# Moving the key transposes of an RWKV recurrence back in TensorE's order, in a hybrid attention, RWKV and mixture-of-experts layer

## Chip, cores and metric

The kernel runs on 1 core of one Trainium2 chip, as one launch. The metric is device time in microseconds; a run's number is the time of that core from the start to the end of the execution. The program is written against a tile framework that orders each engine's instructions when the program is built; on the chip that order is fixed, and semaphores alone hold an instruction back.

## The reference, cut to what matters

One layer on 1024 tokens of width 1024, all in float32:

```python
h = rms_norm(x, norm1_gain)
p = h @ w_in                      # q, k, v of 12 heads; RWKV's r, k, v and LoRAs; two gates
y_att  = dilated_window_attention(q, k, v) @ w_att_out
y_rwkv = rwkv7_time_mix(p_rwkv, ...)          # 8 heads of 64, a scan over the tokens
x = x + (gates[:D] * y_att + gates[D:] * y_rwkv) @ w_out
x = x + hierarchical_moe(rms_norm(x, norm2_gain), ...)   # 32 experts, top 2 in one group

def step(state, inp):             # the scan of rwkv7_time_mix
    r_t, w_t, k_t, v_t, kk_t, b_t = inp
    sa = einsum('bhvk,bhk->bhv', state, -kk_t)
    state = state * w_t + sa[..., None] * b_t + v_t[..., None] * k_t
    return state, einsum('bhvk,bhk->bhv', state, r_t)
```

The scan is computed in chunks of 64 tokens: within a chunk everything is a matrix product, and only the state Z is carried from chunk to chunk.

## The kernel before

**Stages.** The input projection is made tile by tile: a tile is 128 columns of `w_in`, and each takes 48 matmuls of 128 x 128 by 128 x 512 (8 slices of the contraction, two halves of the tokens, and three products of a high and a low part, since the operands are split into two). These are the *dense matmuls* of this text, all issued in `inproj_steps` (L309). Tiles 3 to 14 are RWKV's r, k and v of four head pairs p (three tiles, 144 matmuls, a pair), then come 10 tiles of gates, then the attention's q, k, v.

**The preparation.** `prep(p)` builds, for a head pair p and for each half h of the tokens (so eight *halves* in all), what the recurrence needs, and stores it in DRAM. Its TensorE steps, in source order: projections of decay and rate (L577, L578); key norms (L583) and their spread over rows by transposes (L593); transposes of v (L597); transposes of the keys BK (L647), eight a half; the bonus product (L657, L658); the products BK x AR of each chunk (L672, 32 on the chip a half); and products of the masked result with v (L691). VectorE forms BK in four writes, L631 twice and L634 last in the trace shown; BK has one buffer, so the next half's BK can be written only when this half's transposes and products have read it. The key transposes go through PSUM tiles `pt` to the tile BT (ScalarE copies, L648) and to DRAM as dBT (SyncE's queue, L650). No other step of the preparation reads BT. VectorE cuts the products into cT, Bm and MC with masks (L681, L685, L686).

**The solve and the recurrence.** `solve(q)` inverts the chunks' triangular blocks, 31 steps on VectorE and then small matmuls (L737, L746), of which L737 stands in `tc.high_priority(offset=-400)`. After the preparation the kernel runs the second solve, and then 8 blocks of the recurrence, which load dAR, dMC, dBT and the rest (issued on POOL's queue) and run L851, L859, L867, L874 and L878, with a group norm behind each block (`gnorm`, its transposes are L810). Then come the attention, the merge, and the experts.

**Fillers.** The dense matmuls are generators in a list `fillers`. `fill(n)` issues the next n of them at that place of the source. In a half of `prep` there are 16 in front of L593, 2 + 2 + 14 between L597 and L647, and 28 behind that, 62 in all; at the start of each `prep` the rest of the pair's 144 is issued. So the source mixes 62 dense matmuls into every half.

**Order.** The source order is only a preference. Every instruction gets a number by its place in the source; when the program is built the framework steps through an estimate of the execution, and whenever an engine is free it takes, of the instructions of that engine that are ready, the one with the lowest number. `tc.high_priority(offset=-400)` adds 400 to the numbers inside it. A dense matmul far later in the source is therefore taken as soon as nothing earlier is ready.

The lines that the change touches, L643 to L650; LP is 0:

```python
            for jj in range(2):
                pt = pb([2, 2, 128])
                for j in range(2):
                    for c in range(2):
                        with tc.high_priority(offset=-LP):
                            nc.tensor.transpose(pt[:, j, c], BK[:, 2 * jj + j, 128 * c:128 * c + 128], ident)
                nc.scalar.activation(BT[:, 2 * jj:2 * jj + 2], pt, AF.Copy)
                fill(FQ)
            stq.dma_start(dBT[j0:j0 + 4, :, p].rearrange("j q m -> q j m"), BT.rearrange("q j c k -> q j (c k)"))
```

Of the kernel before, what the change touches and what calls it, by code (L numbers as in the profile page):

```python
# [26 lines left out]
FT, FS, FP, FA, GL = 20, 6, 2, 18, 10  # L27
FI, FQ, TP, FR, SQ, SG, SB, UJ, QW, QL, QT, QJ = 14, 2, 1, 16, 1, 0, 1, 1, 1, 0, 0, 1
FB = 14
LP, LB, LR, PF, MP, QB, GB, NY = 0, 0, 0, 1, 0, 1, 2, 2  # L30
DILS = (1, 4, 16)
NEG = -1e30
N_EXP = 32
# [1755 lines left out]
```

## Time and profile before

| | |
|---|---|
| median of 3 runs | 1712.75 us (1712.74 to 1716.41) |
| the profiled execution | 1709.74 us |
| its span, first to last instruction | 1708.0 us |
| TensorE busy | 1643.0 us, 96% of the span |
| VectorE busy | 1201.2 us, 70% |
| ScalarE busy | 873.0 us, 51% |
| mean granted clock of TensorE | 0.986 of full speed |

PE is TensorE, PEld its weight loads, DVE VectorE, ACT ScalarE, POOL GpSimd, SP SyncE. A row of a timeline has the start, the duration (both us), the engine and line, the operation, the tile written and the tiles read, the shape and, behind x, how many like instructions it merges; in brackets stands the idle time of the engine ahead of it and what ended it. Matmuls overlap, so the pace of a run of them is the distance of their starts, not the duration. A row of a table by stage has the stretch, its length, busy time and number of instructions of each engine, the granted clock of TensorE and the share and rate of the DMA engines. A row of waits has the waiting engine and line, what it waited for, the sum in us, how many times, and the longest.

### The profile page before, as it was taken

The page shows a single profiled execution, that of the slowest core. Times are in us where ns is not written, and L with a number is a line of the kernel's source. Part 1 is how long each engine was busy: PE and PEld are TensorE (multiplying, and loading weights), DVE is VectorE, ACT ScalarE, POOL GpSimd, SP SyncE. Part 2 cuts the span into 40 slices and gives each one's busy share as a digit, 9 for nine tenths or more (in the row PEclk, how much of TensorE's full clock was granted, in tenths as well). Part 3 has the DMA queues.
Part 4 walks back from the last instruction along what each step waited for, and adds up shares of the span by engine and source line. Part 5 has one row for each costly group of instructions (what it writes and reads, how often), then busy time and mean ns, then how long its engine had stood idle before and what let it go on. Part 6 is the DMA issues. An engine that isn't in the chain of part 4 may idle for free. (4 is left out here: it accounts for less than half of the span.)

```text
span 1708.0 us, 25910 instructions
## 1 busy us (share of the span) xinstructions
PE 1643.0 (96%) x9419; PEld 1307.3 (77%) x9420; DVE 1201.2 (70%) x2191; ACT 873.0 (51%) x1317; POOL 304.1 (18%) x338
## 2 busy tenths in 40 slices
PE   8999999999998999999999999799999999999996
PEld 6677777787776777777777777578888888888884
DVE  5648798793663445434326856699999999998985
ACT  4524443423221334343433122388888888887774
POOL 0100102223431011000112211212222212221211
PEclk9999999999998999999999999899999999999998
DMA  8334324474752121111128573689999999999993
GB/s 298 120 91 133 121 87 142 136 258 146 231 176 68 38 69 56 50 41 53 69 74 301 210 266 136 234 274 373 379 374 370 376 366 377 372 361 366 366 376 102
DMA packets 138411, 360.34 MB, mean 211 GB/s; under 512 B 15792, under 2 KB 57344, under 8 KB 138276
## 3 DMA queue, kind: packets, MB, share of 16 engines
q1 hardware_dynamic: 116140, 297.89, 47.9%
q0 software_dynamic: 17936, 56.33, 11.6%
q10 hardware_dynamic: 4200, 4.40, 0.8%
q8 instruction: 76, 1.25, 0.3%
q14 instruction: 59, 0.48, 0.1%
HBM read 304.39 MB, written 62.29 MB: 215 GB/s over the span
## 5 line engine op out<-in xcount | busy, mean ns | idle before, releaser
L1605 PE MATMUL pb<-u,xTh 128*128 128x512 f32 x1040 | 343.2, 405 | 0.5 <-ACT xTh L1600 0.5
L309 PE MATMUL pa<-xlo,wh 128*128 128x512 f32 x736 | 302.3, 411 | 0.0
L309 PE MATMUL pa<-xhi,wh 128*128 128x512 f32 x736 | 299.3, 407 | 2.9 <-DVE qT L937 1.4
L309 PE MATMUL pa<-xhi,wl 128*128 128x512 f32 x736 | 297.0, 404 | 2.3 <-DVE wl L280 2.3
L1605 PEld LDWEIGHTS pb<-u,xTh 128*128 128x128 f32 x1040 | 193.7, 189 | 41.8 <-ACT xTh L1600 1.3
L1605 PE MATMUL pb<-u,xTl 128*128 128x512 f32 x520 | 210.5, 405 | 0.0
L309 PEld LDWEIGHTS pa<-xhi,wh 128*128 128x128 f32 x736 | 140.1, 190 | 36.0 <-DVE qT L937 1.8
L309 PEld LDWEIGHTS pa<-xlo,wh 128*128 128x128 f32 x736 | 139.9, 190 | 34.9 <-issue 4.0
L309 PEld LDWEIGHTS pa<-xhi,wl 128*128 128x128 f32 x736 | 140.0, 190 | 34.1 <-DVE wl L280 3.2
L1491 DVE TENSOR_TENSOR u<-fs,u 128x1024 fp32r<-128x1024 f32 x133 | 157.3, 1219 | 8.9 <-ACT u L1490 5.9
L1491 DVE TENSOR_TENSOR u<-mix,u 128x1024 fp32r<-128x1024 f32 x128 | 151.5, 1218 | 11.3 <-ACT u L1490 9.1
L1490 ACT ACTIVATE u<-fs 128x1024 fp32r<-128x1024 f32 x133 | 137.6, 1057 | 18.0 <-PE pb L1605 11.6
L1490 ACT ACTIVATE u<-mix 128x1024 fp32r<-128x1024 f32 x128 | 133.3, 1056 | 16.6 <-PE pb L1605 8.6
L1605 PE MATMUL pa<-u,hTh 128*128 128x512 f32 x496 | 138.9, 401 | 0.1
L1012 DVE SCALAR_TENSOR_TENSOR Sb<-pb,rqk,bias 128x128 f32<-128x128 f32 (+1 forms) x96 | 35.5, 407 | 120.8 <-PE pb L1011 101.3
L1584 POOL DMA_INDIRECT out<-row,tba x30 | 82.4, 2747 | 198.0 <-ACT u L1490 174.6
L1605 PEld LDWEIGHTS pb<-u,xTl 128*128 128x128 f32 x520 | 98.0, 188 | 18.1 <-DVE xTl L1601 0.6
L1605 PEld LDWEIGHTS pa<-u,hTh 128*128 128x128 f32 x496 | 90.5, 188 | 20.7 <-DVE u L1491 1.0
L1491 DVE TENSOR_TENSOR u<-raw,u 128x1024 fp32r<-128x1024 f32 x83 | 98.3, 1219 | 7.8 <-ACT u L1490 6.8
L278 ACT ACTIVATE wh<-wr 128x1024 fp32r<-128x1024 f32 x49 | 51.8, 1056 | 96.3 <-PE pa L309 76.1
L1490 ACT ACTIVATE u<-raw 128x1024 fp32r<-128x1024 f32 x83 | 86.2, 1056 | 11.8 <-PE pb L1605 6.9
L1578 POOL DMA_INDIRECT xin<-dH,tbl x32 | 37.9, 1185 | 251.1 <-PE pb L1599 231.8
(428 smaller groups left out, 2972.5 us busy)
## 6 DMA issues: line engine op xcount, KB each, us to landing
wr<-in_w_in SPq DMA_DIRECT2D x49, 512.0 KB, 3.4
fs<-in_w_expert_up SPq DMA_DIRECT2D x46, 512.0 KB
mix<-in_w_expert_gate SPq DMA_DIRECT2D x44, 512.0 KB, 12.0
fs<-in_w_expert_gate SPq DMA_DIRECT2D x44, 512.0 KB, 11.7
fs<-in_w_expert_down SPq DMA_DIRECT2D x43, 512.0 KB, 3.8
mix<-in_w_expert_down SPq DMA_DIRECT2D x42, 512.0 KB, 11.7
mix<-in_w_expert_up SPq DMA_DIRECT2D x42, 512.0 KB
raw<-in_w_expert_down SPq DMA_DIRECT2D x32, 512.0 KB, 12.8
```

The source lines that it names most:

```text
L278: nc.scalar.activation(wh, wr, AF.Copy)
L309: nc.tensor.matmul(ps, a[:, k, :], b[:, k, hs], start=(n == 0), stop=(n == 23))
L1012: nc.vector.scalar_tensor_tensor(Sb[:, hh, 0:nk], pS[:, 0:nk], u.rn[:, 0, i, hh:hh + 1], u.bias[:, hh, 256 - nk:], op0=ALU.mult, op1=ALU.add)
L1490: nc.scalar.activation(hi, raw, AF.Copy)
L1491: nc.vector.tensor_tensor(lo, raw, hi.bitcast(F32), op=ALU.subtract)
L1578: nc.gpsimd.indirect_dma_start(out=dst, out_offset=None, in_=src, in_offset=bass.IndirectOffsetOnAxis(ap=idx, axis=0), bounds_check=S - 1, ...
L1584: nc.gpsimd.indirect_dma_start(out=out, out_offset=bass.IndirectOffsetOnAxis(ap=idx, axis=0), in_=src, in_offset=None, compute_op=ALU.add)
L1605: nc.tensor.matmul(ps, x, w, start=first, stop=last)
```

## The change

The constant LP goes from 0 to 400. The 64 key transposes get numbers that are 400 higher: among the instructions that are ready, TensorE takes them after everything up to 400 places later in the source, the dense matmuls of later tiles included. Their ScalarE copies and stores keep their own numbers, but depend on the transposes.

```diff
-LP, LB, LR, PF, MP, QB, GB, NY = 0, 0, 0, 1, 0, 1, 2, 2
+LP, LB, LR, PF, MP, QB, GB, NY = 400, 0, 0, 1, 0, 1, 2, 2
```

## Rows read from the trace of the kernel before

**Rows 1.** Page, busy time of each engine over the span.

```profile
PE 1643.0 (96%) x9419; PEld 1307.3 (77%) x9420; DVE 1201.2 (70%) x2191; ACT 873.0 (51%) x1317; POOL 304.1 (18%) x338
```

**Rows 2.** Table by stage: preparation, recurrence, and the stretch behind it.

```profile
117.00:351.00 234.00, 223.27 (x1432) 180.38 (x1433) 192.03 (x468) 101.88 (x181) 31.57 (x51) 0.99 0.38 123
...
395.00:513.00 118.00, 116.67 (x1642) 92.73 (x1641) 68.37 (x195) 35.48 (x69) 45.32 (x66) 1.00 0.61 192
513.00:530.00 17.00, 10.06 (x36) 7.62 (x35) 8.48 (x23) 1.69 (x2) 5.61 (x6) 0.70 0.38 108
```

**Rows 3.** Waits of TensorE, 117 to 351 us, the longest.

```profile
PE pb L647 <- DVE BK L634: 7.5, 6, 1.6
```

**Rows 4.** Timeline around the transposes of the second half.

```profile
159.10 0.68 DVE L634 SCALAR_TENSOR_TENSOR BK<-kk,iP 128x512 f32<-128x512 f32 x1
...
159.93 1.06 PE L647 MATMUL pb<-ident,BK 128*128 128x128 f32 x8 [1.38 <-DVE BK L634]
...
160.75 0.48 PE L657 MATMUL pb<-sg,onr 128*128 128x512 f32 x1
...
161.05 1.06 ACT L648 ACTIVATE BT<-pb 128x512 f32<-128x512 f32 x2
...
161.47 3.50 PE L672 MATMUL pb<-AR,BK 64*128 64x128 f32 x32
...
162.84 1.22 DVE L280 TENSOR_TENSOR wl<-wr,wh 128x1024 fp32r<-128x1024 f32 x1
...
164.09 0.93 DVE L681 TENSOR_TENSOR cT<-pb,cv 32x128 f32<-32x128 f32 x3
...
165.23 0.40 PE L309 MATMUL pa<-xhi,wh 128*128 128x512 f32 x1
...
166.40 0.40 PE L309 MATMUL pa<-xhi,wl 128*128 128x512 f32 x1
```

**Rows 5.** L309 alone, from the start to L647 of five halves.

```profile
0.00:133.60 133.60, 70.93 (x289) 0.99 0.50 167
0.00:186.80 186.80, 103.17 (x415) 0.99 0.47 158
0.00:212.00 212.00, 117.91 (x473) 0.99 0.46 154
0.00:238.60 238.60, 135.44 (x543) 0.99 0.45 149
0.00:340.90 340.90, 198.36 (x781) 0.99 0.42 141
```

**Rows 6.** Timeline, the second solve: YT and the first product that reads it.

```profile
383.35 2.13 DVE L724 STREAM_TRANSPOSE YT<-M 128x1024 f32<-128x1024 f32 x1
...
391.43 0.24 PE L737 MATMUL pb<-YT,LW 32*32 32x32 f32 x2
```

**Rows 7.** Timeline: transposes of the third half, first BK write of the fourth.

```profile
186.84 1.06 PE L647 MATMUL pb<-ident,BK 128*128 128x128 f32 x8 [1.58 <-DVE BK L634]
...
209.27 0.75 DVE L631 TENSOR_TENSOR BK<-tc,iP 128x256 f32<-128x256 f32 x2
```

**Rows 8.** Timeline: the first product of the recurrence.

```profile
395.45 0.96 PE L851 MATMUL pb<-Z,ARs 64*64 64x64 f32 x16
```

**Rows 9.** Waits of VectorE for TensorE, 117 to 351 us.

```profile
DVE cT L681 <- PE pb L672: 2.9, 5, 0.7
...
DVE tb L660 <- PE pb L658: 1.2, 2, 0.6
```

**Rows 10.** Timeline behind the recurrence, TensorE.

```profile
521.78 1.12 PE L810 MATMUL pb<-ident,gyc 128*128 128x128 f32 x4 [5.50 <-POOL gyc L805]
524.34 0.79 PE L309 MATMUL pa<-xhi,wh 128*128 128x512 f32 x1 [1.44 <-DVE qT L937]
524.93 0.63 PE L309 MATMUL pa<-xlo,wh 128*128 128x512 f32 x1
...
528.34 0.63 PE L309 MATMUL pa<-xhi,wh 128*128 128x512 f32 x1
```

## Prediction

> **What bounds the kernel now.** I read the page first, then a table by stage, then who waited for whom in the stage that holds the change, then the timeline of one half. In [rows 1] TensorE is busy for 1643.0 of 1708.0 us, so a change of order that removes no TensorE work can only win back its idle time, 65 us in all. [rows 2] cut the early part into stages. The stage of the change (117 to 351 us, eight "halves": four head pairs p, two halves of the sequence each) leaves TensorE idle for 234.00 - 223.27 = 10.7 us; the recurrence stage (395 to 513) for 1.3 us; the short stretch behind it (513 to 530) for 6.9 us, at a mean granted clock of 0.70.
>
> Who is waited for in the first of these: [rows 3] put 7.5 us of the 10.7, in six waits, on the first key transpose of a half (L647), which waits for the last write of BK on VectorE (L634). [rows 4] show one of these: VectorE ends BK at 159.10 + 0.68, the transposes start at 159.93 after 1.38 us of idle TensorE, then come the two bonus matmuls (L657, L658), then the BK x AR products (L672), then dense matmuls again. The reader is to see two things there. The dense matmuls stand behind the whole block, although they need none of it. And the instruction next in line that matters, L672, reads BK as well.
>
> So a half is a loop through two resources: TensorE work, and a chain BK, L672, masks on VectorE, L691, the next half's projections, the next BK. Dense matmuls fill what the chain leaves free.
>
> **The change, part by part.** It alters no instruction, only the place of 64 transposes (8 a half) in TensorE's order, and with them the 16 ScalarE copies (L648) and 8 SyncE stores of dBT, which follow their transposes. Nothing is added or removed.
>
> *What leaves the front of the block.* Eight transposes take from 159.93 to the next instruction at 160.75: 0.82 us a half, 8 x 0.82 = 6.6 us in all. They must still run, so TensorE's total stays; only the chain can get shorter.
>
> *What happens to the 7.5 us of waiting.* Products L672 keep their priority and need the same write of BK, and the dense matmuls that TensorE runs at that moment are far later in the source than L672 (next paragraph), so L672 is the next to be chosen when BK is ready. I expect the same wait with L672's name on it: 0 us won. The bounds are 0 and 7.5 us (if something else took its place); I take 0, since [rows 4] show L672 right behind. The rows show TensorE idle ahead of L647 with dense work queued behind it. The Trainium skill, "TensorE: Matmul & The Clock Gate", section "Part 2: What happens when you issue a matmul", says that matmuls stay in program order and that only weight loads are pulled ahead; by that rule, which speaks against reading the 7.5 us as a gain, a wait changes its owner and the sum for it is 0, without it 7.5 us.
>
> *Where the transposes go.* The offset puts each one 400 instructions later in preference. A half issues by the source 118 instructions of its own, 62 dense matmuls and some 14 for their evacuation and weights, 194 together; two halves with the 20 dense matmuls between two preps are slightly over 400. So a transpose yields to dense matmuls up to some 138 later in the source. How far the dense stream is already ahead is a count: by the source 144 + 34 = 178 dense matmuls stand before the first half's transposes, 432 + 34 = 466 before those of the fifth, 576 + 96 = 672 before the last; [rows 5] have 289, 543 and 781, so it is ahead by 111, 77 and 109 (93 in the third half: 415 against 322). The transposes then fall back by about 138 less this, 27 to 61 dense matmuls. One takes (166.40 - 165.23) / 5 = 0.234 us [rows 4], so 6 to 14 us. An existing instruction with the same offset agrees: YT is finished at 383.35 + 2.13 = 385.48, and its first user L737 runs at 391.43, 6 us later [rows 6].
>
> *What waits for them there.* BK has one buffer, so the next half's first write (L631) waits for them: from 186.84 to 209.27 there are 22.4 us [rows 7], and 473 - 415 = 58 dense matmuls [rows 5]. Mostly covered; the fifth half, at 61 before the extra instructions of the solve (which shorten its reach), is near the edge. The stores of dBT are read back for the recurrence, whose first product stands at 395.45 [rows 8]; the last half's transposes, put back by 138 - 109 = 29 to at worst 138 dense matmuls (7 to 32 us after 341), end 20 us before that, so the store and the load behind them have time. On ScalarE the two copies cost 1.06 us [rows 4] and may stand before the next half's key norm (L588): between 0 and 1.06 us a half. I take 0, since ScalarE is busy in 101.88 of 234 us [rows 2]; in all 8 halves it would be 8.5 us.
>
> *What the shorter block gives the chain.* The products start up to 0.82 us earlier. That helps only where VectorE stood waiting for them. [rows 9]: it waited for L672 2.9 us in five waits (0.7 at most, so each is below 0.82), and 1.2 us for L658. In the other three halves it did not wait; in [rows 4] it is at a weight split (L280) when the products arrive and turns to them at 164.09 only. Below: 0 us. Above: 6.6 us. I take 2.9 us, the waits on L672; those on L658 stay, because the bonus matmuls may now fall behind the products.
>
> *Where it comes out.* TensorE loses no work, so 2.9 us must be taken from idle time. The dense matmuls left over, 2.9 / 0.234 = 12, are used up later, and the only idle time of size is behind the recurrence: 5.50 us before L810 and 1.44 before the next dense matmul [rows 10]. There is room for them.
>
> The sum on the profiled execution, span 1708.0 and 1709.74 with what lies around it: 1709.74 - 2.9 = 1706.8. The median of the runs shown, 1712.75, is 3.0 above that execution; on it, 1709.9.
>
> **The rivals.**
> *A, the forecast:* a small gain, 1709.9; its own range is 1707.6 to 1713.
>
> *B, the whole block comes off the chain.* For it: three of the six waits are in halves where VectorE is full only because of how its queue happened to be ordered; with products 0.82 us earlier the order may change too. Then 6.6 us, and the idle time behind the recurrence nearly closes. Behind that idle time the rows show the lower of the two clock levels: from 524.93 to 528.34 eight dense matmuls take 0.426 us each instead of 0.234 [rows 10]; ten at that pace cost 1.9 us, which would be saved. 1712.75 - 8.5 = 1704.3. The Trainium skill, same page, section "Part 1: The HAM clock gate (the "warmup" mystery)", says that the throttled clock is the default and activity releases it; the trace agrees here (0.70 over 513 to 530, 0.426 us a matmul), and by it this part of B follows from the idle time alone. Against B: VectorE is busy for 192.03 of 234 us [rows 2], with little room to start earlier.
>
> *C, the single BK buffer takes it back (slower).* Place: L631 of the next half. It decides from where the transposes fall back by more than 58 dense matmuls. If 400 places reach a fifth further than I count, that is 25 dense matmuls more: the fifth half falls back by 86 and waits (86 - 58) x 0.234 = 6.6 us, the third and fourth by about 72, 3.3 us each. 13.2 - 2.9 = 10.3 us on the chain, 1723.0. TensorE would run dense matmuls meanwhile, but these are then missing in the recurrence, where idle time grows. For it: the edge is near. Against it: [rows 6], where 6 us were enough.
>
> *D, nothing happens:* the transposes come right behind the products, L672 inherits wait and chain, 1712.75.
>
> **How the numbers follow.** A 0.50, B 0.25, C 0.19, D 0.06. The likeliest is A, 1709.9. The range: B's 1704.3 at the lower end, and above as far into C as 8 in 10 asks (half of its price, some 5 us): 1704 to 1718. What a measurement can tell from no change is 0.3%, 5.1 us; A and D lie within it, B is faster, C slower: 0.25, 0.56, 0.19.
>
> **What would show it.** Right: L647 in the middle of dense runs, after L672; the wait on BK L634 in the name of L672 and still 6 to 8 us; "cT waits for L672" below 1 us; the first L851 1 to 4 us earlier; less than 5.5 us before the last L810. Wrong: L631 waiting for L647 (C); the wait on BK gone, or L851 earlier by over 5 us (B). I would be wrong altogether if the new order moved anything after 530 us: no term here reaches that far, and the sum assumes that all later stages only shift.

## The result and the profile after

The changed kernel takes 1723.76 us (median of 4 runs, 1720.88 to 1724.94); the kernel before, run beside it, 1712.74 us (4 runs, 1712.38 to 1716.41). The ratio is 1.006, with a 95% interval of 1.0043 to 1.0078: slower by 0.6%, clear of 1, and above the forecast range. The profiled execution took 1723.83 us, its span is 1722.1 us. The busy row of its page and its table by stage, to be held against [rows 1, 2]:

```profile
PE 1642.9 (95%) x9419; PEld 1313.8 (76%) x9420; DVE 1202.7 (70%) x2191; ACT 874.3 (51%) x1317; POOL 302.4 (18%) x338
```

```profile
117.00:351.00 234.00, 224.80 (x1413) 182.65 (x1414) 183.24 (x448) 101.16 (x175) 30.57 (x52) 0.97 0.35 118
395.00:513.00 118.00, 108.08 (x1554) 89.61 (x1552) 73.14 (x199) 32.91 (x63) 45.79 (x70) 0.97 0.63 200
```

TensorE's busy time is the same to 0.1 us. The preparation even has a little less idle time (9.2 us against 10.7). The loss shows in the recurrence's stretch: 118.00 - 108.08 = 9.9 us idle, where it was 1.3.

Fixed stretches mix stages once these have moved, so the next table cuts at events: the first matmul of the recurrence (L851, 395.45 before, 412.26 after) and the first of the attention behind it (L969, 543.63 and 553.60). Its columns are those of [rows 2]. The kernel before:

```profile
117.00:395.50 278.50, 267.77 (x1681) 215.54 (x1681) 227.13 (x545) 112.92 (x196) 45.84 (x77) 0.99 0.43 141
395.50:543.60 148.10, 139.84 (x1730) 111.05 (x1730) 79.46 (x222) 38.95 (x73) 50.93 (x72) 0.97 0.54 168
```

The changed kernel:

```profile
117.00:412.30 295.30, 284.20 (x1754) 230.60 (x1754) 230.14 (x549) 117.00 (x200) 44.64 (x78) 0.98 0.41 136
412.30:553.60 141.30, 121.60 (x1658) 101.32 (x1658) 77.23 (x218) 36.09 (x69) 50.59 (x72) 0.93 0.55 169
```

Here the time can be seen. Ahead of the recurrence TensorE does 1754 - 1681 = 73 matmuls more and needs 295.3 - 278.5 = 16.8 us more. Behind that point it has 72 fewer to do, but saves only 148.1 - 141.3 = 6.8 us, since its idle time rises from 8.3 to 19.7 us. 16.8 - 6.8 = 10.0 us, which is L969's delay. The 73 are dense matmuls. Counts of L309 alone, the changed kernel up to the transposes of the fourth half, to those of the last, and to L851 (before: 473 and 781 [rows 5]), and below them the kernel before up to L851:

```profile
0.00:221.40 221.40, 129.88 (x513) 0.98 0.44 149
0.00:365.20 365.20, 227.34 (x891) 0.98 0.42 140
0.00:412.20 412.20, 265.40 (x1047) 0.98 0.44 149
...
0.00:395.40 395.40, 245.10 (x974) 0.99 0.46 152
```

Why they run early is in the timeline of the second half, which answers to [rows 4]:

```profile
166.41 0.68 DVE L634 SCALAR_TENSOR_TENSOR BK<-kk,iP 128x512 f32<-128x512 f32 x1
...
167.55 0.27 PE L647 MATMUL pb<-ident,BK 128*128 128x128 f32 x1
167.58 0.48 PE L309 MATMUL pa<-xhi,wl 128*128 128x512 f32 x1
167.89 0.49 PE L647 MATMUL pb<-ident,BK 128*128 128x128 f32 x3
...
168.46 0.27 PE L647 MATMUL pb<-ident,BK 128*128 128x128 f32 x1
168.49 0.48 PE L657 MATMUL pb<-sg,onr 128*128 128x512 f32 x1
168.81 0.40 PE L658 MATMUL pb<-at,onr 128*128 128x512 f32 x1
169.13 2.05 PE L672 MATMUL pb<-AR,BK 64*128 64x128 f32 x18
172.26 1.89 PE L672 MATMUL pb<-AR,BK 64*128 64x128 f32 x14 [1.08 <-DVE tb L660]
174.08 0.90 PE L647 MATMUL pb<-ident,BK 128*128 128x128 f32 x3
```

The transposes sit among dense matmuls, as meant. But L657, L658 and L672 did not stay where they were: they follow at once behind the first transpose of the *second* tile `pt`, and only the last three transposes come behind them. All PSUM tiles named pb here come from one pool of five buffers, which is handed out in source order: a tile later in the source gets no slot while an earlier one has not got its own. So the late transposes hold back the bonus and the products, in every half: by the counts of L309, the first L672 of a half comes 35 to 53 dense matmuls later in the first seven halves, and 113 later in the last. The products of the last half, before and then in the changed kernel, and the first L737 of the second solve in the changed kernel:

```profile
342.48 3.50 PE L672 MATMUL pb<-AR,BK 64*128 64x128 f32 x32
...
367.03 3.50 PE L672 MATMUL pb<-AR,BK 64*128 64x128 f32 x32
...
409.59 1.20 PE L737 MATMUL pb<-YT,LW 32*32 32x32 f32 x64 [1.67 <-DVE YT L724]
```

L647 and L672 of the last half begin 24 us later, and the solve's YT is ready 24 us later too (at 409.4 us, 385.5 before). L851 comes only 16.8 us later, mostly because there were 6 us of slack: L737 used to run 6 us behind YT [rows 6], and now TensorE waits for YT.

What the recurrence lacks then is seen in two timelines of TensorE late in it. The kernel before:

```profile
470.78 0.50 PE L309 MATMUL pa<-xlo,wh 128*128 128x512 f32 x1
...
471.58 0.39 PE L309 MATMUL pa<-xlo,wh 128*128 128x512 f32 x1
472.14 0.93 PE L851 MATMUL pb<-Z,ARs 64*64 64x64 f32 x16 [0.17 <-issue]
```

The changed kernel, and the clock in the stretch that follows:

```profile
483.66 0.69 PE L867 MATMUL pb<-UVs,BTs 128*64 128x64 f32 x16 [0.39 <-ACT UVs L860]
484.19 1.10 PE L878 MATMUL pb<-UVs,MCs 128*64 128x64 f32 x16
486.75 0.93 PE L851 MATMUL pb<-Z,ARs 64*64 64x64 f32 x16 [1.47 <-issue]
487.96 0.34 PE L859 MATMUL pb<-Rs,TTs 64*64 64x64 f32 x1 [0.28 <-issue]
```

```profile
484.00:488.00 4.00, 2.25 (x46) 0.99 0.97 260
488.00:492.00 4.00, 3.76 (x50) 0.50 1.06 374
```

Before, dense matmuls fill what the chain of Z leaves free; after, none is left, the waits stand open, and the granted clock falls to the lower level (1.2 GHz). That none is left is a count of L309 again, first in the kernel before from L851 on, then in the changed kernel:

```profile
395.40:519.00 123.60, 48.57 (x154) 1.00 0.60 189
...
412.20:480.00 67.80, 24.95 (x81) 1.00 0.66 208
480.00:530.00 50.00, 0.00 (x0) 0.89 0.55 168
```

974 + 154 and 1047 + 81 are both 1128: so many dense matmuls stand ahead of the one that waits for qT (L937). Before, the last of them starts at 515.9 us, close to the end of the recurrence; after, at 475.6, and the 50 us behind it have none. TensorE's waits from L851 to L969 in the changed kernel, the longest:

```profile
PE pb L810 <- POOL gyc L805: 8.3, 1, 8.3
PE pb L867 <- ACT UVs L860: 3.6, 9, 0.4
PE pb L851 <- issue: 2.5, 2, 1.5
```

The 8.3 us are the wait of [rows 10], which was 5.50:

```profile
531.62 1.11 PE L810 MATMUL pb<-ident,gyc 128*128 128x128 f32 x4 [8.31 <-POOL gyc L805]
534.18 0.80 PE L309 MATMUL pa<-xhi,wh 128*128 128x512 f32 x1 [1.44 <-DVE qT L937]
```

From L969 to the end the profiled execution takes 4.1 us more than that of before (1168.5 against 1164.4). In the experiments this part takes 1163 to 1179 us, in no order that follows the theories below, and the profile of before was one of its quicker executions (1709.74, medians 1712.7 to 1714.5). I don't count it.

### The profile page after: what moved, and what is told of

It is laid out like the page before. It is cut to its first block, busy times and chain, and to the rows that moved or that the text cites. A ratio compares the mean times of both kernels' runs of the same rounds, so it can differ in the third digit from the quotient of the medians.

```text
span 1722.1 us, 25899 instructions
## 1 busy us (share of the span) xinstructions
PE 1642.9 (95%) x9419; PEld 1313.8 (76%) x9420; DVE 1202.7 (70%) x2191; ACT 874.3 (51%) x1317; POOL 302.4 (18%) x338
## 5 line engine op out<-in xcount | busy, mean ns | idle before, releaser
L309 PE MATMUL pa<-xhi,wh 128*128 128x512 f32 x736 | 299.5, 407 | 4.6 <-DVE gs L384 2.2
L309 PE MATMUL pa<-xlo,wh 128*128 128x512 f32 x736 | 301.7, 410 | 0.0
L309 PE MATMUL pa<-xhi,wl 128*128 128x512 f32 x736 | 298.3, 406 | 1.4 <-DVE wl L280 1.4
L309 PEld LDWEIGHTS pa<-xhi,wh 128*128 128x128 f32 x736 | 140.9, 191 | 37.3 <-DVE gs L384 2.3
L309 PEld LDWEIGHTS pa<-xlo,wh 128*128 128x128 f32 x736 | 140.7, 191 | 35.0 <-issue 4.0
L309 PEld LDWEIGHTS pa<-xhi,wl 128*128 128x128 f32 x736 | 140.4, 191 | 33.9 <-DVE wl L280 2.6
L1490 ACT ACTIVATE u<-fs 128x1024 fp32r<-128x1024 f32 x133 | 137.6, 1056 | 18.0 <-PE pb L1605 11.4
```

Of the source, the lines that this page charges most:

```text
L309: nc.tensor.matmul(ps, a[:, k, :], b[:, k, hs], start=(n == 0), stop=(n == 23))
L1490: nc.scalar.activation(hi, raw, AF.Copy)
```

## The experiments

All ratios are against runs of the kernel before on the same chip.

**Theory P** (shared PSUM slots): as above, the late transposes hold back bonus and products through the pool. **Theory K** is rival C: BK's one buffer delays the next half.

The first four runs, e1 to e4, free the products from the late transposes. In the first two the transposes get a pool of their own, with offset 0 (e1, the control) and 400 (e2):

```diff
-    psB = ctx.enter_context(tc.tile_pool(name="psB", bufs=5, space=PSUM))
+    psB = ctx.enter_context(tc.tile_pool(name="psB", bufs=4, space=PSUM))
+    psT = ctx.enter_context(tc.tile_pool(name="psT", bufs=1, space=PSUM))
...
-                pt = pb([2, 2, 128])
+                pt = psT.tile([128, 2, 2, 128], F32, name="pk")
```

> Control: offset 0, but the key transposes write a PSUM pool of their own with one slot, and the shared pool keeps four of its five. Both theories expect the time of the kernel before, 1712.7 us, within 4 us: a slot less can move a few steps, nothing is late.

> Offset 400 with the transposes' own PSUM pool. Theory P (the shared pool hands out its slots in source order, so a late transpose holds back the bonus and the products BK x AR behind it): the transposes are as late as in the changed kernel, but the products stand where they stood before, so the time is that of the control within 4 us, or up to 5 us below it, since the block has lost 0.82 us a half. Theory K (the single buffer of BK, rival C of the prediction): BK is released as late as in the changed kernel, so the 11 us stay, about 1724.

The third (e3) takes each tile's slot in time, with its first transpose; the fourth (e4), at offset 0, moves the transposes' loop and the store of dBT in the source to just before the store of dMC:

```diff
-                        with tc.high_priority(offset=-LP):
+                        with tc.high_priority(offset=0 if j + c == 0 else -LP):
```

> Offset 400 for three of the four transposes of each PSUM tile, 0 for the first one, which takes the slot. One pool as before. Theory P: the slot queue is not held, the products stand near their old place, 1709 to 1717 us. Theory K: the last transposes still read BK as late as in the changed kernel, about 1724.

> Offset 0, but the loop of the transposes is moved in the source behind the products and the masks. The slots are then asked for in that order too. This is the change as the prediction pictured it (products first, transposes right behind): by its sum 2.9 us below the kernel before, 1709.8, between 0 and 6.6 us won. Theories P and K both expect no loss; a loss of over 5 us would be against both.

Measured: e1, the control, 1725.56 us, 1.0064 (1.0051 to 1.0077); e2 1733.41, 1.0104 (1.0085 to 1.0123); e3 1732.55, 1.0100 (1.0085 to 1.0116); e4 1727.74, 1.0072 (1.0052 to 1.0093). In all four the products were in time, within 15 dense matmuls of their old place, and L851 stood behind 974 or 975 dense matmuls again. So P's account of *who held whom back* is right, but the time did not come back: no run came where P or K had put it, and as a theory of the time, P alone fell. The control, in which nothing is late, lost 11 us, as much as the change itself, and late transposes cost 8 us more on top of it (e2 against e1). Of those 8 us, 7 show between L852 and L970, the L851 and L969 of these kernels: 156.0 us in e2 against 148.9 in e1, at a mean clock of 0.93 against 0.97. In e4 the cost stands ahead of L851:

```profile
117.00:410.30 293.30, 281.11 (x1681) 0.94 0.40 134
```

e4 runs the same 1681 matmuls ahead of L851 as before, in 293.3 us instead of 278.5, with no more idle time to speak of (12.2 us against 10.7), at a mean granted clock of 0.94 instead of 0.99: TensorE's clock went to its lower level in five places of the preparation, against two before. So another order can by itself cost as much as the change. In the changed kernel that is not what is paid ahead of L851: its 73 dense matmuls more are 73 x 0.234 us [rows 4] = 17.1 us, all of the 16.8.

The second four leave pools and source alone and choose which halves are late.

**Theory F** (fillers): what costs is that the *last* half's products, and so L851, come later, and 73 dense matmuls are used up ahead of the recurrence. **Theory G:** each half pays for its own late transposes and products.

```diff
# e5: the last half alone
+                        with tc.high_priority(offset=-(LP if (p, h) == (3, 1) else 0)):
# e6: the first six halves
+                        with tc.high_priority(offset=-(LP if p < 3 else 0)):
# e7: offset 400 everywhere, and
+            BK = p1.tile([128, 4, 256], F32, name="BK", bufs=2)
# e8: offset 200 everywhere
```

> Offset 400 for the transposes of the last half alone, 0 for the other seven; in program order the first seven halves stand as in the kernel before and the recurrence's first matmul comes behind 1047 dense matmuls, as in the change (974 before). Theory F (the last half's products, held back, let 73 more dense matmuls be used up ahead of the recurrence, which then has none left for its own waits): nearly the whole loss, 1720 to 1725 us, with TensorE idle for 8 to 11 us in the recurrence. Theory G (each half pays for its own late transposes and products, some 1.4 us a half): 1713 to 1716 us. Theory K (the next half's keys wait for the one buffer of BK; the last half has none behind it): as before, 1711 to 1716 us.

> Offset 400 for the first six halves, 0 for the last two, so that the recurrence's first matmul comes behind 974 dense matmuls again, as before. Theory F: near the kernel before, 1711 to 1716 us, and under 3 us idle in the recurrence. Theory G: six eighths of the loss, 1719 to 1722 us. Theory K: most of the loss too, 1719 to 1723 us.

> The change with two buffers for BK; TensorE's order is that of the change. Theory K (the single buffer): back to 1711 to 1716 us. Theories F and G: no gain, 1721 to 1726 us, first L851 still near 412 us.

> Offset 200 in place of 400 in all eight halves; it puts the transposes at the same place as before in seven halves within 10 dense matmuls, and the recurrence's first matmul at about 975. Theories F, G and K all give the time before, 1711 to 1717 us. If any reshuffling of TensorE's order costs several us by itself (clock dips at other places), 1718 us or more.

Measured: e5, the last half alone, 1726.92 us, 1.0081 (1.0054 to 1.0108); e6, the first six, 1713.78, 1.0004 (0.9990 to 1.0017); e7, two BK buffers, 1723.14, 1.0062 (1.0041 to 1.0082); e8, offset 200, 1713.19, 0.9996 (0.9984 to 1.0009). e6, e7 and e8 came where F had put them, e5 2 us above F's range. Six late halves cost nothing and one late half costs it all: G and K are out. A second BK buffer changes nothing. The table from 117 us to L851 and on to L969, first for the last half alone, then for the first six halves:

```profile
117.00:413.70 296.70, 283.98 (x1753) 0.99 0.41 136
413.70:555.70 142.00, 122.67 (x1658) 0.93 0.54 168
```

```profile
117.00:396.80 279.80, 268.25 (x1680) 0.98 0.42 139
396.80:544.20 147.40, 139.08 (x1732) 0.98 0.55 171
```

The one has nearly the changed kernel's lines, the other nearly those of before, in matmuls, idle time and clock.

The last four try F from other sides: late transposes with products in time (own pool, the last half alone), late products with transposes in time, a larger and a smaller offset for the last half alone.

```diff
# e9: e2's pools, with e5's line
# e10: offset 0 for the transposes, and around L672
+                        with tc.high_priority(offset=-(400 if (p, h) == (3, 1) else 0)):
# e11, e12: e5 with LP = 800 and with LP = 300
```

> Keys' transposes in a PSUM pool of their own, offset 400 for those of the last half alone: its products come on time (dense count 794), its transposes 97 dense matmuls later, the recurrence's first matmul at 975. Its control is the run with a pool of their own and offset 0, 1725.6 us. Theory F (the late products cost the time, not the late transposes): as the control, 1723 to 1728 us. If late transposes cost time by themselves: 1730 to 1735 us, as with offset 400 for all halves in that pool.

> All key transposes at offset 0, the products L672 of the last half alone at offset 400: transposes on time (790), products 117 to 130 dense matmuls later than before, the recurrence's first matmul at 1064. Theory F: as the change, 1721 to 1728 us, with some 10 us idle in the recurrence. If the late transposes were what costs: 1711 to 1716 us.

> Offset 800 for the last half's transposes alone: transposes and products at 976, the recurrence's first matmul at 1122, so 148 dense matmuls more than before are gone ahead of it, twice the change's 73. Theory F: the idle time in the recurrence doubles, 1730 to 1740 us. If the loss came from the shift in the last half alone and not from the missing dense matmuls, some 1724 us again.

> Offset 300 for the last half's transposes alone: its transposes and products come 46 dense matmuls later than before, but the recurrence's first matmul still stands at 975. Theory F (what counts is how many dense matmuls are left for the recurrence): 1711 to 1717 us. If the lateness of the products counts by itself: about half of the loss, 1718 to 1721 us.

Measured: e9 1731.05 us, 1.0089 (1.0072 to 1.0107); e10 1735.24, 1.0110 (1.0089 to 1.0131); e11 1744.89, 1.0174 (1.0154 to 1.0193); e12 1719.64, 1.0024 (1.0000 to 1.0049).

e11, the larger offset, went the way that F said, and further: 1744.89 us, 5 above F's 1730 to 1740. L851 stands behind 1122 dense matmuls, and the stretch from L851 to L969 has 137.6 - 110.1 = 27.5 us of idle time (8.3 before, 19.7 after the change):

```profile
435.30:572.90 137.60, 110.08 (x1583) 0.84 0.52 162
```

The less is left, the less comes back: the 73 matmuls taken away by the change shortened this stretch by 6.8 us, the 75 taken away beyond that by 3.7, at a lower mean clock (0.84 against 0.93).

e10, late products alone, cost more than the change (F expected 1721 to 1728), so late transposes aren't needed for the loss; TensorE idles 20.5 us from L851 to L969, as after the change, but at a mean clock of 0.85 instead of 0.93:

```profile
421.90:569.10 147.20, 126.67 (x1642) 0.85 0.49 157
```

In e9 the products of the last half stand in time and its transposes 25 us behind them. Timeline of TensorE (lines are one further down in this kernel):

```profile
350.03 1.16 PE L673 MATMUL pb<-AR,BK 64*128 64x128 f32 x8
...
351.54 2.68 PE L673 MATMUL pb<-AR,BK 64*128 64x128 f32 x24
...
379.00 0.27 PE L648 MATMUL pk<-ident,BK 128*128 128x128 f32 x1
```

This is P's mechanism in one view: with slots of their own, late transposes hold nothing back. L969 came at 553.1 us, 2.7 behind the control, where the change is 10.0 behind the kernel before; but the whole took 5.5 us more than the control, outside F's 1723 to 1728 and inside the 1730 to 1735 of the rival, that late transposes cost time by themselves. The rest is behind L969, among it 14 us at the lower clock from 828 us on, which no other profile has. Whether late transposes bring that about is not shown, so this rival stays open.

e12, the smaller offset, missed F's 1711 to 1717 and came inside the 1718 to 1721 of the rival, that the lateness of the products counts by itself. Its L851 stands behind 975 dense matmuls and at 397.1 us, nearly as before, but from there to L969 it takes 154.1 us instead of 148.1. Its profile shows where, first in TensorE's timeline, then in a table of 4 us each (length, busy time, matmuls, granted clock, DMA share and rate):

```profile
393.39 1.53 PE L737 MATMUL pb<-YT,LW 32*32 32x32 f32 x64 [1.59 <-DVE YT L724]
```

```profile
394.00:398.00 4.00, 4.00 (x55) 0.50 0.38 135
398.00:402.00 4.00, 4.00 (x77) 0.50 0.18 66
402.00:406.00 4.00, 4.00 (x22) 0.50 0.37 131
406.00:410.00 4.00, 4.00 (x74) 0.79 0.18 66
```

Products later by 46 dense matmuls make the solve later, L737 waits 1.59 us for YT, and the 14 us behind it run at the lower level. By the pace of dense matmuls at the two levels (0.426 and 0.234 us, [rows 10, 4]) that costs an estimated 14 x (1 - 0.234 / 0.426) = 6 us. Of its six runs five took 1718.55 to 1723.24 us at mean clocks of 0.979 to 0.982, and one 1710.66 us at 0.985: the same program can also cost nothing, though there is no trace of that run to show whether it was this stretch that held its clock. So F names where the change's 10 us go, but late products can cost time even when as many dense matmuls are left as before. No version was measurably faster than the kernel before.

## Why the prediction was wrong

*Where the transposes go* was right for the earlier halves: in the four of them in [rows 5] they fell back by 39 to 44 dense matmuls, in the fourth by 513 - 473 = 40 (27 to 61 were forecast). In the last, the one that counts, it was 891 - 781 = 110, near the worst case of 138 and not near 29.

*The step that failed* is "Products L672 keep their priority ..., so L672 is the next to be chosen when BK is ready". The number of L672 was kept, its PSUM slot was not: it queued behind the transposes' second tile. Under "What waits for them there" I looked at BK's buffer, the stores and ScalarE, and not at the tile that the transposes write. In the first six halves this cost nothing (e6); that the chain had room there is my reading, and no run isolates it. In the last it delayed the chain to the recurrence by 24 us at the transposes and 16.8 us at L851.

*"No term here reaches that far"*, said of anything after 530 us, failed with it: L969 comes 10.0 us later. I took TensorE's total as what bounds, so that dense matmuls run earlier are only moved. They are also the stock that the recurrence lives on: 17.1 us of it were spent ahead of L851, and 6.8 us came back.

*The waits.* "The wait on BK L634 in the name of L672" did not come: part of it stayed with L647 (4.6 us of the 7.5 [rows 3]), L672 waited for tb instead, VectorE's wait for the bonus product (L658) rose from 1.2 us [rows 9] to 7.2, and VectorE's wait for L672 fell from 2.9 us to 2.5 only, where below 1 was expected. Waits of the changed kernel, 117 to 351 us:

```profile
DVE tb L660 <- PE pb L658: 7.2, 3, 4.5
PE pb L647 <- DVE BK L634: 4.6, 4, 1.7
DVE cT L681 <- PE pb L672: 2.5, 3, 1.1
```

The gain of A and B, earlier products, was thus nowhere to be had: they came later in every half.

*Rival C* had the time (1723.0) and the last link (dense matmuls "missing in the recurrence, where idle time grows"), but not the cause: two BK buffers give 1723.14, and the half that decides is the last, which has no next half to delay. Its agreement in time is chance.

*What stays open:* why the control with a pool of its own is 11 us slower than the kernel before (between the two profiles it is 16.4 us; 6.0 of these stand ahead of L851, at a mean clock of 0.98 instead of 0.99, and most of the rest behind L969), why late transposes with products in time cost more than that control (e2, e9), and how much late products cost by themselves (e12). No run with transposes as late as the change's in the last half got the time back. So it is the order of the instructions that shows the shared pool holding the products back, and not a time.

## What to carry to other kernels

Giving an instruction a lower priority delays whatever gets its buffer after it: look at the pool of the tile it *writes*, and at every later tile of that pool, not only at those who read its result. Work that can go anywhere is a stock; ask which stage has nothing else to fill its waits, and count how much of the stock is left when that stage begins. And try such a change half by half: here the first six halves of it are free and worthless, and the last costs everything.

## What the hardware showed that I had not expected

The clock could be lost behind short waits, and the wait alone did not decide it. It fell to its lower level behind a wait of 1.59 us ahead of small matmuls (e12, three stretches at 0.50 above), and behind waits of 0.39, 1.47 and 0.28 us among small matmuls without dense ones in between (the changed kernel, 488 us). Behind the similar wait of 1.38 us [rows 4], followed by transposes, products and dense matmuls, it stayed at 1.00 in the kernel before. And it stayed at 1.00 in the changed kernel, too, behind the 1.67 us ahead of the same 64 matmuls of L737 as in e12 (1.00 over 408 to 428 us). At that place e5 has 1.71 us and no fall, e10 1.64 us and a fall. So the same wait in the same place can cost its own length or, by the estimate above, some 6 us more, and no run here shows what decides. Kernels with the same work and nearly the same idle time lie up to 15 us apart at L851 (e4). The Trainium skill, "TensorE: Matmul & The Clock Gate", section "A second HAM failure mode: psum-queue depth-cycling", describes a kernel in which frequent short idle times between groups of matmuls make the clock go back and forth; the trace agrees (0.50 from 488 to 492 us, 1.00 again from 495 to 505 us).
